# A decoder trunk's squared-ReLU MLP: reordering its first, middle and last steps

## The chip, the cores and the metric

The kernel runs on one core of one Trainium2 chip. The metric is the device time of one execution in microseconds. A core has five engines that run side by side, each working through its own instructions strictly in the order in which they were queued: TensorE (PE in the profile, with its weight loads as PEld), VectorE (DVE), ScalarE (ACT), GpSimd (POOL) and SyncE (SP), which here only issues DMAs. They wait for one another through semaphores. What an engine does after an instruction that waits has to wait too, even if its own data are there.

## The reference

The input is 1024 tokens of 1024 features. There are two layers. Each adds three terms to the residual stream x: a token mixer (a convolution block in layer 0, forgetting attention, "FoX", in layer 1), cross-attention into 256 memory tokens, and the MLP. The change is about the MLP, what comes just before it (the memory attention) and what comes just after the first one (FoX):

```python
def rmsnorm(x, g):
    y = x * lax.rsqrt(jnp.mean(x * x, axis=-1, keepdims=True) + RMS_EPS)
    return y * g

def sqrelu_mlp(h, w1, w2):                       # 1024 -> 4096 -> 1024
    return jnp.square(jax.nn.relu(h @ w1)) @ w2

# per layer l
x = x + memory_cross_attention(rmsnorm(x, norm_mem_g[l]), ...)
h = rmsnorm(x, norm_ff_g[l])
x = x + sqrelu_mlp(h, ff_w1[l], ff_w2[l])
# before layer 1: k, v, gates from rmsnorm(x, kv_norm_g) @ kvf_w; q from rmsnorm(x, norm_mix_g[1]) @ fox_wq
```

## The kernel before

**Layout and precision.** Features lie on the 128 partitions: x is kept as 16 tiles `X[:, c, half]` of 128 x 512 (8 chunks of features by 2 halves of the tokens). Each product is made three times, to keep accuracy: an operand is split into a rounded high part (made by ACT, a copy to the rounded type) and a low part, the rest (made by DVE: source minus high part, line 153, `low`). Three matmuls, low by high, high by low and high by high, then go into the same bank of PSUM (`passes`, `product`).

**The MLP as a list of steps.** `mlp` (line 581) does each of its two products with the seven-product scheme for 2 by 2 blocks (Strassen-Winograd): instead of eight products of quarter blocks it needs seven, and pays with sums of quarters. `steps` (line 636) is one list of 226 entries (weight group g, which weight piece b11, b21, t1 ..., which quarter of the operand a11, a12, s1 ..., which PSUM bank, its pool). One step is 12 matmuls: 4 chunks by 3 passes. Steps 0 to 15 are done the plain way, for groups 0 and 1, while the quarter sums s1 to s4 of x are not there yet: steps 0 to 7 use the first half of the tokens (a11, a12), steps 8 to 15 the second (a21, a22). From step 16 on, 14 steps serve two groups: groups 2 to 15 make the inner activation u (steps 16 to 113), groups 16 to 31 multiply it by the second weight (steps 114 to 225).

**The order of the work is written out by hand.** `at(n, f)`, `at_once(n, f)` and `at_end(n, f)` put a piece of work before, first before, or after step n. The loop at line 1011 goes through the steps and issues, for each n: the work put before it, the high part of the weight of step n+5 (ACT, line 628), its low part for step n+4 (DVE, line 632), the 12 matmuls (line 1026), and the work put after it. The context `in_order` (line 995 to 1031) fixes this order on every engine, SP among them. Weights of the seven-product scheme are themselves sums: `combine` (POOL, line 622) makes t1 to t4 of a group from its raw pieces, t1 = b12 - b11, t2 = b22 - t1, and so on. The raw pieces of a group come in two loads, `load_raw(g, 0)` with b11 and b21 and `load_raw(g, 1)` with b12 and b22, into two buffers for each of the two.

**The first steps.** The sum of squares of the second half of the tokens is made when the loop is about to begin (line 1010: 8 Squares on ACT, 7 additions on DVE, line 188). After step 0, PE takes its mean over the features (line 163), DVE and POOL make the inverse root, and after step 1 PE spreads it over the partitions (line 172). From step 2 on, DVE scales the second half (line 674), ACT and DVE split it, and POOL makes the quarter sums in place, four instructions for each chunk c = 0 to 3 (`sum_second`, line 689). Their high parts (ACT, line 704) stand at step 6 + c and their low parts (DVE, line 709) at 7 + c; s4 follows at 14 and 15. After step 15 the memory of x is given up for 16 buffers "u" (`open_up`), and ACT takes the first results out of PSUM into them (line 842).

**The middle.** u and its quarter sums go through memory in HBM: `store` and `low_inner` write them, `load_inner` reads them back as operands of the second product, in four parts f = 0 to 3 of four groups each. a11 and a12 are stored already split (high and low). s1 to s4 and a22 are stored once and split again when read: `high_of_inner` (ACT, line 910) and `low_of_inner` (DVE, line 914). For the first part, f = 0, the loads stand at steps 102, 104, ... 114, in the order a11, a12, s2, s3, s1, a22, s4, and the splits of s2 at 108 and 110, of s1 at 112 and 113, of s4 at 116 and 117. The raw weights b12 and b22 of groups 16 and 17 are loaded at 110 and 111. In the second product, a bank holds first a11's product; ACT copies it (`copy_first`, line 924) before a12's product is added into it, which is why steps 116 and 117 wait for the copies of 114 and 115.

**The last steps, and FoX.** In the last 14 steps (212 to 225) the results are added to x (DVE, line 934), squared (ACT, line 970) and summed (DVE, line 978) for the next norm. The mean of the first half is taken after step 222, its spread after 223. `fox_layer` (line 1035) then scales and splits the first half (line 216 on DVE, 218 on ACT, 153 on DVE), and multiplies it by the first pieces of wk and fox_wq (line 259) and by the gate weights; the second half of x follows. `projections` (line 1157) goes on from there; it asks for the first piece of wv when it is at the second entry of its list.

## Time and profile before

| | |
|---|---|
| median of 3 timed runs (lowest to highest) | 2849.24 us (2848.0 to 2851.68) |
| the profiled execution: time, span | 2853.82 us, 2852.0 us |
| PE busy, of the span | 2749.8 us, 96% |
| DVE, ACT, POOL busy | 71%, 45%, 28% |
| matmuls of the two MLPs (line 1026) | 5424, 1253.8 us |
| mean granted TensorE clock | 0.988 |

The stages follow one another on PE: convolution and memory matrices to 517 us or so, memory attention, the first MLP (713 to 1361 us), FoX (to about 1980 us), memory attention, the second MLP (2185 to 2836 us), the last norm. A row of a group reads: line, engine, operation, tile written <- tiles read, shapes, count | busy time, mean duration in ns of one | idle time of the engine just before these instructions, and what ended it. Idle time counts only on the engine that bounds a stage; here that is PE almost everywhere. A row of a stretch (from:to in us) reads: length, busy time of PE, PEld, DVE, ACT and POOL with the number of instructions, then the TensorE clock that was granted (1.00 is full), the share of time in which the DMA engines were busy, and what they moved.

### The profile page before, as it was taken

The page shows a single profiled execution, that of the slowest core. Times are in us where ns is not written, and L with a number is a line of the kernel's source. Part 1 is how long each engine was busy: PE and PEld are TensorE (multiplying, and loading weights), DVE is VectorE, ACT ScalarE, POOL GpSimd, SP SyncE. Part 2 cuts the span into 40 slices and gives each one's busy share as a digit, 9 for nine tenths or more (in the row PEclk, how much of TensorE's full clock was granted, in tenths as well). Part 3 has the DMA queues.
Part 4 walks back from the last instruction along what each step waited for, and adds up shares of the span by engine and source line. Part 5 has one row for each costly group of instructions (what it writes and reads, how often), then busy time and mean ns, then how long its engine had stood idle before and what let it go on. Part 6 is the DMA issues. An engine that isn't in the chain of part 4 may idle for free.

```text
span 2852.0 us, 36295 instructions
## 1 busy us (share of the span) xinstructions
PE 2749.8 (96%) x12968; PEld 2265.0 (79%) x12968; DVE 2038.1 (71%) x3295; ACT 1276.7 (45%) x2293; POOL 809.7 (28%) x537
## 2 busy tenths in 40 slices
PE   8999999999899999999799999989999999999998
PEld 6777877888688878888588888878887788878886
DVE  5999983644775576777788888875545865677776
ACT  5112143533465553334466666673433555543332
POOL 0000000000666544774000000000000766635763
PEclk9999999999999999999999999999999999999999
DMA  6334463222165576552222221243213355565651
GB/s 217 118 118 133 136 201 118 86 89 85 42 216 178 189 285 209 211 199 96 67 62 72 64 64 54 68 135 103 94 56 104 117 201 179 198 228 203 225 197 62
DMA packets 165429, 390.68 MB, mean 137 GB/s; under 512 B 17265, under 2 KB 46193, under 8 KB 164993
## 3 DMA queue, kind: packets, MB, share of 16 engines
q1 hardware_dynamic: 165248, 388.37, 40.4%
q8 instruction: 102, 1.67, 0.2%
q14 instruction: 79, 0.64, 0.1%
HBM read 270.79 MB, written 113.31 MB: 135 GB/s over the span
## 4 chain that ended last, share of the span: by engine, by line
PE 74%; DVE 11%; ACT 5%; DMA 4%; issue 3%; POOL 2%; SPq 0%; DVEq 0%; POOLq 0%; ACTq 0%
PE mm L1026 36%; PE mm L259 27%; PE mm L1182 5%; DVE op L153 2%; POOL x L689 2%; DVE x L398 1%; DVE w L153 1%; PE mm L1268 1%; DVE x L1237 1%; PE mm L1280 1%; PE mm L1281 1%; ACT x L1242 1%; DMA raw<-mqk 1%; DVE both L390 1%; PE mm L1232 1%
## 5 line engine op out<-in xcount | busy, mean ns | idle before, releaser
L1026 PE MATMUL mm<-op,w 128*128 128x512 f32 x5424 | 1253.8, 393 | 31.5 <-DVE w L153 11.1
L1026 PEld LDWEIGHTS mm<-op,w 128*128 128x128 f32 x5424 | 1027.0, 190 | 255.0 <-ACT m L924 11.5
L259 PE MATMUL mm<-op,wh 128*128 128x512 f32 x1056 | 329.1, 393 | 0.7 <-DVE op L153 0.7
L153 DVE TENSOR_TENSOR w<-r,w 128x512 fp32r<-128x512 f32 x264 | 267.4, 1017 | 33.5 <-ACT w L628 33.5
L203 POOL TENSOR_TENSOR r<-v,mhalf 128x4 f32<-128x4 f32 (+1 forms) x17 | 18.8, 1106 | 928.1 <-DVE v L201 928.1
L628 ACT CAST w<-r 128x512 fp32r<-128x512 f32 x264 | 162.7, 622 | 259.8 <-PE mm L1026 195.1
L259 PEld LDWEIGHTS mm<-op,wh 128*128 128x128 f32 x1056 | 198.9, 189 | 45.7 <-DVE op L153 4.0
L1182 PE MATMUL mm<-op,wh 128*128 128x512 f32 x736 | 230.3, 394 | 0.0
L153 DVE TENSOR_TENSOR w<-t,w 128x512 fp32r<-128x512 f32 x180 | 178.4, 1003 | 65.0 <-ACT w L628 64.8
L259 PE MATMUL mm<-op,wl 128*128 128x512 f32 x528 | 210.0, 399 | 12.7 <-ACT op L218 8.3
L622 POOL TENSOR_TENSOR t<-r,t 128x512 f32<-128x512 f32 x120 | 194.2, 1618 | 95.1 <-DVE w L153 53.8
L156 ACT CAST wh<-raw 128x1024 fp32r<-128x1024 f32 x96 | 100.8, 1051 | 197.2 <-PE mm L259 121.9
L628 ACT CAST w<-t 128x512 fp32r<-128x512 f32 x180 | 112.0, 622 | 151.8 <-PE mm L1026 133.4
L622 POOL TENSOR_TENSOR t<-r,r 128x512 f32<-128x512 f32 x60 | 95.1, 1585 | 290.8 <-DMA r<-in_ff_w 209.8
L934 DVE TENSOR_TENSOR x<-mm,x 128x512 f32<-128x512 f32 x160 | 109.5, 684 | 94.3 <-PE mm L1026 77.6
L830 POOL TENSOR_TENSOR u<-u 128x512 f32<-128x512 f32 x112 | 160.3, 1455 | 6.5 <-ACT u L840 3.0
L1182 PEld LDWEIGHTS mm<-op,wh 128*128 128x128 f32 x736 | 138.8, 189 | 26.6
L259 PE MATMUL mm<-op,xsh 128*128 128x512 f32 x512 | 158.0, 393 | 0.1
L1182 PE MATMUL mm<-op,wl 128*128 128x512 f32 x368 | 154.7, 420 | 2.5 <-DVE wl L153 2.5
L156 ACT CAST pth<-mm 128x512 fp32r<-128x512 f32 (+1 forms) x224 | 105.9, 495 | 109.0 <-PE mm L546 80.8
L398 DVE SCALAR_TENSOR_TENSOR x<-d,par,x 128x512 f32<-128x512 f32 x232 | 154.6, 746 | 0.0
L1242 ACT ACTIVATE x<-x,nb 128x128 f32<-128x128 f32 (+7 forms) x128 | 99.5, 778 | 109.6 <-DVE nb L1240 102.9
(179 smaller groups left out, 4754.3 us busy)
## 6 DMA issues: line engine op xcount, KB each, us to landing
r<-in_ff_w SPq DMA_DIRECT2D x128, 512.0 KB, 4.0
op<-ua SPq DMA_DIRECT2D x80, 512.0 KB, 6.9
us<-u SPq DMA_DIRECT2D x128, 256.0 KB, 3.0
op<-us SPq DMA_DIRECT2D x64, 512.0 KB, 5.5
raw<-mvo SPq DMA_DIRECT2D x32, 512.0 KB, 3.3
ua<-ul SPq DMA_DIRECT2D x64, 256.0 KB, 2.1
ua<-uh SPq DMA_DIRECT2D x60, 256.0 KB, 2.2
raw<-in_pw SPq DMA_DIRECT2D x24, 512.0 KB, 4.8
```

Source lines behind the costliest of these rows:

```text
L153: dve.tensor_tensor(lo, src, hi.bitcast(F32), op=ALU.subtract)
L156: act.copy(hi, src)
L259: pe.matmul(out_ps, x, y, start=i == 0, stop=i == len(terms) - 1)
L398: dve.scalar_tensor_tensor(out[s], d[:, j : j + n], w, y, op0=ALU.mult, op1=ALU.add)
L622: pool.tensor_tensor(t, raws[g, x], raws[g, y], op=ALU.subtract)
L628: act.copy(highs[n][0], raws[steps[n][:2]])
L689: pool.tensor_tensor(out, x1, x2, op=op_)
L830: eng.tensor_tensor(u[g, x], y1, y2, op=op_)
L934: dve.tensor_tensor(v, sums[key], v, op=ALU.add)
L1026: pe.matmul(sums[key], y, z, start=first and i == 0, stop=n == last_of[key] and i == len(terms) - 1, skip_group_check=True,)
L1182: pe.matmul(t, x, y, start=n == 0, stop=n == len(terms) - 1)
L1242: act.activation(x[:, :n], x[:, :n], AF.Exp, bias=nb, accum_out=rs)
```

## The change

It has these parts.

1. **Early sum of squares.** `mem_attention` squares each chunk of the second half as soon as it is final and returns the sum (`seconds`); the sum at line 1010 is gone.
2. **Steps 0 to 15.** Group 1 goes first and group 0 second; in steps 8 to 15 group 0 comes first (its weights are still there from steps 4 to 7) and group 1 last, with its four pieces in another order. The two raw buffers are now tied to g % 2 by name. The raw weights of group 2 are loaded at 4 and 5 (2 and 3 before), those of group 3 at 10 and 12 (10 and 10).
3. **Copies paced by the quarter sums.** The high parts of chunk c = 0 to 3 stand at steps 7, 10, 12 and 14, the low parts one step later; all of s4 at 15. Group 3's t1 and t2 are made at 15 instead of 12.
4. **Middle.** For the first part (groups 0 to 3), s1 and s2 are split when they are made, at steps 29 to 40, and stored as high and low (`ue`), in place of the plain stores; they are read back split, with two loads for one. Their splits at 108 to 113 are gone. Until they are split they stay in their u buffers. Of the last group of the first product, s3 moves from 113 and 114 to 115.
5. **Next norm within the last steps.** For the first MLP, the scaling and splitting of the first half for FoX is put into steps 224 and 225 and after 225 (`start_fox`, `ending`).
6. **FoX** asks for the first piece of wv right after the second half has been scaled and split.

```diff
+    def add_squares(acc, ch):
+        sq = nrm.tile([P, HALF], F32, name="sq", tag="t", bufs=4)
+        act.activation(sq, ch, AF.Square)
+        if acc is None:
+            return sq
+        dve.tensor_tensor(acc, acc, sq, op=ALU.add)
+        return acc
...
                     add_to_x(m, sl, t)
+                    if sl is HALVES[1]:
+                        sums = add_squares(sums, X[:, m, sl])
+            return sums
...
+        ue = {x: dram.tile([P, 2, 4, HALF], F32, name=f"ue{x}{layer}") for x in ("s1", "s2")}
...
-                r = pw.tile([P, NCH, P], F32, name=f"r{j}")
+                r = raw_tiles[g % 2][j]
...
-            for g in range(2):
+            for g in (1, 0):
                 steps += [
...
-            for g in (1, 0):
-                for b, x, c in (("b11", "a21", "c21"), ("b12", "a21", "c22"), ("b21", "a22", "c21"), ("b22", "a22", "c22")):
-                    if g:
-                        again[len(steps)] = {"b11": 4, "b21": 5, "b12": 6, "b22": 7}[b]
-                    steps.append((g, b, x, (g, c), pm if g else ps))
+            seconds_of = (("b11", "a21", "c21"), ("b12", "a21", "c22"), ("b21", "a22", "c21"), ("b22", "a22", "c22"))
+            for b, x, c in seconds_of:
+                again[len(steps)] = {"b11": 4, "b21": 5, "b12": 6, "b22": 7}[b]
+                steps.append((0, b, x, (0, c), pm))
+
+            for b, x, c in (seconds_of[k] for k in (0, 2, 1, 3)):
+                steps.append((1, b, x, (1, c), ps))
...
-                second["r"] = rms_of_sums(second["acc"], RMS_EPS)
+                second["r"] = rms_of_sums(seconds, RMS_EPS)
...
-            for c in range(4):
-                at(6 + c, highs_of_sums, c, ("s2", "s3", "s1"))
-                at(7 + c, lows_of_sums, c, ("s2", "s3", "s1"))
-            at(14, open_operand, "s4")
-            for c in range(4):
-                at(14 + c // 2, highs_of_sums, c, ("s4",))
-                at(15, lows_of_sums, c, ("s4",))
-            at(2, load_raw, 2, 0)
-            at(3, load_raw, 2, 1)
+            for c, n in enumerate((7, 10, 12, 14)):
+                at(n, highs_of_sums, c, ("s2", "s3", "s1"))
+                at(n + 1, lows_of_sums, c, ("s2", "s3", "s1"))
+            at(15, open_operand, "s4")
+            for f in (highs_of_sums, lows_of_sums):
+                for c in range(4):
+                    at(15, f, c, ("s4",))
+            at(4, load_raw, 2, 0)
+            at(5, load_raw, 2, 1)
             at(10, load_raw, 3, 0)
-            at(10, load_raw, 3, 1)
+            at(12, load_raw, 3, 1)
...
-                        at(b - 4 + late, combine, g + i, t)
+                        at(b - 1 if g + i == 3 else b - 4 + late, combine, g + i, t)
...
+            for n, g in ((29, 0), (31, 1), (37, 2), (39, 3)):
+                for i, x in enumerate(("s2", "s1")):
+                    split_inner_at(n + i, g, x)
...
-                        at(b + 13 + i, inner_sums, g + i, NEW[:3], dve)
-                        at(b + 15, inner_sums, g + i, NEW[3:], dve)
+                        at(b + 13 + i, inner_sums, g + i, NEW[:2], dve)
+                        at(b + 15, inner_sums, g + i, NEW[2:], dve)
...
+            def split_before(f, x):
+                return f == 0 and x in ue
...
-                    if x in SPLIT_FIRST:
+                    if x in SPLIT_FIRST or split_before(f, x):
                         for i in range(2):
-                            nc.sync.dma_start(t[:, i].bitcast(F32), ud[x][:, i, k, :])
+                            nc.sync.dma_start(t[:, i].bitcast(F32), (ud if x in SPLIT_FIRST else ue)[x][:, i, k, :])
...
+            def begin_next():
+                for n, f in ending(second["rb"]):
+                    at(end - n, f)
+            if ending is not None:
+                at(b + 12, begin_next)
...
-                second["acc"] = sum_of_squares([X[:, c, HALVES[1]] for c in range(NCH)])
...
+    def start_fox(rb, hs):
+        h = {}
+        def first(c):
+            if c == 0:
+                hs.extend(operands())
+            h[c] = nrm.tile([P, HALF], F32, name="h", tag="t", bufs=4)
+            dve.tensor_tensor(h[c], X[:, c, HALVES[0]], rb, op=ALU.mult)
+            act.copy(hs[c][0][:, HALVES[0]], h[c])
+        def second(c):
+            hi, lo = (y[:, HALVES[0]] for y in hs[c])
+            low(lo, h.pop(c), hi)
+        todo = [(first, 0)]
+        for c in range(1, NCH):
+            todo += [(first, c), (second, c - 1)]
+        todo.append((second, NCH - 1))
+        at = [2] * 4 + [1] * 4 + [0] * (len(todo) - 8)
+        return [(n, partial(f, c)) for n, (f, c) in zip(at, todo)]
...
-                normalize(hs, None, HALVES[0], firsts)
...
                 normalize(hs, None, HALVES[1], rb)
+                ws.append(weights(a["wv"][0], gain="kv"))
...
-            if 0 < j < len(order) - 1:
+            if 1 < j < len(order) - 1:
```

More of the change, by code (lines that the diff above doesn't have):

```diff
@@ L552, in mem_attention @@
             late = None
+            sums = None
             for sl in HALVES:
@@ L578, in mem_attention, with mlp @@
                     add_to_x(m, sl, t)
-    def mlp(layer, copy=None):
+                    if sl is HALVES[1]:
+                        sums = add_squares(sums, X[:, m, sl])
+            return sums
+    def mlp(layer, seconds, copy=None, ending=None):
         nonlocal X, xpool
@@ L605, in operand @@
                 return [(t[:, 0, i, :], t[:, 1, i, :]) for t in ts for i in range(2)], ts
+            raw_tiles = [
+                [pw.tile([P, NCH, P], F32, name=f"r{i}{j}", bufs=1) for j in range(2)] for i in range(2)
+            ]
             def load_raw(g, j):
@@ L811, in low_inner @@
                 low(lo, u[g, x], hi)
+                if x in ue:
+                    del u[g, x]
                 for i, y in enumerate((hi, lo)):
-                    nc.sync.dma_start(ud[x][:, i, g, :], y.bitcast(F32))
+                    nc.sync.dma_start((ue if x in ue else ud)[x][:, i, g, :], y.bitcast(F32))
             def split_inner_at(n, g, x):
@@ L833, in store_rest @@
                 for x in ("a22", "s1", "s2", "s3", "s4"):
-                    store(g, x)
+                    if g >= 4 or x not in ue:
+                        store(g, x)
             def first_outputs(g, names, square):
@@ L845, in mlp @@
             at_end(15, open_up)
-            at_end(15, first_outputs, 0, ("c11", "c12"), False)
-            at(16, first_outputs, 1, ("c11", "c12"), False)
-            at(16, first_outputs, 1, ("c21", "c22"), False)
-            at(17, first_outputs, 1, ("c11", "c12", "c21", "c22"), True)
-            at(18, first_outputs, 0, ("c21", "c22"), False)
-            at(18, first_outputs, 0, ("c11", "c12", "c21", "c22"), True)
-            for g, n in ((1, 18), (0, 23)):
+            at_end(15, first_outputs, 1, ("c11", "c12"), False)
+            at(16, first_outputs, 0, ("c11", "c12"), False)
+            at(16, first_outputs, 0, ("c21", "c22"), False)
+            at(17, first_outputs, 0, ("c11", "c12", "c21", "c22"), True)
+            at(18, first_outputs, 1, ("c21", "c22"), False)
+            at(18, first_outputs, 1, ("c11", "c12", "c21", "c22"), True)
+            for g, n in ((0, 18), (1, 23)):
                 at(n, inner_sums, g, NEW, pool)
@@ L946, in mlp @@
                 for x, ns in (("s2", (8, 10)), ("s1", (12, 13)), ("s4", (16, 17)), ("s3", (19, 20)), ("a22", (22, 23))):
-                    for j, n in enumerate(ns):
+                    for j, n in enumerate(() if split_before(f, x) else ns):
                         at(lb + n, high_of_inner, f, x, j)
@@ L991, in mlp @@
             at_end(b + 11, spread_second)
+            def begin_next():
[3 more added lines that the diff above has]
+                at(b + 12, begin_next)
             with in_order():
                 store_x(0)
-                for g in range(2):
+                for g in (1, 0):
                     for j in range(2):
@@ L1009, in mlp @@
                     fetch_low(n)
-                second["acc"] = sum_of_squares([X[:, c, HALVES[1]] for c in range(NCH)])
                 for n in range(len(steps) + 1):
-                    for f in urgent[n] + before[n]:
+                    for f in chain(urgent[n], before[n]):
                         f()
@@ L1032, in mlp, with fox_layer @@
         return second["rb"], accs[1]
-    def fox_layer(xd, firsts, seconds):
+    def start_fox(rb, hs):
[15 more added lines that the diff above has]
+        return [(n, partial(f, c)) for n, (f, c) in zip(at, todo)]
+    def fox_layer(xd, hs, seconds):
         nonlocal X, xpool
@@ L1291, in trunk @@
         conv_layer(pm, chain(*(memory_matrices(*pools, l) for l in range(2))))
-    mem_attention(0)
+    seconds = mem_attention(0)
     xd = dram.tile([P, NCH, S], F32, name="xd")
-    firsts, seconds = mlp(0, copy=xd)
-    fox_layer(xd, firsts, seconds)
-    mem_attention(1)
-    firsts, seconds = mlp(1)
+    first_normalized = []
+    firsts, seconds = mlp(0, seconds, copy=xd, ending=lambda rb: start_fox(rb, first_normalized))
+    fox_layer(xd, first_normalized, seconds)
+    seconds = mem_attention(1)
+    firsts, seconds = mlp(1, seconds)
     for sl in HALVES:
```

3 lines of the change are left out of this document (1 added, 2 removed).

## The prediction

> **What bounds the kernel now.** First the page: which engine has no time left.
>
> ```profile
> span 2852.0 us, 36295 instructions
> ...
> PE 2749.8 (96%) x12968; PEld 2265.0 (79%) x12968; DVE 2038.1 (71%) x3295; ACT 1276.7 (45%) x2293; POOL 809.7 (28%) x537
> ```
>
> PE bounds it, and no matmul is removed, so the change can only give back PE's idle time and the slow matmuls that follow it. The groups of PE say where it idles in the stages that the change touches:
>
> ```profile
> L1026 PE MATMUL mm<-op,w 128*128 128x512 f32 x5424 | 1253.8, 393 | 31.5 <-DVE w L153 11.1 <-ACT m L924 10.6 <-ACT u L842 4.8
> ...
> L259 PE MATMUL mm<-op,wl 128*128 128x512 f32 x528 | 210.0, 399 | 12.7 <-ACT op L218 8.3 <-DVE wl L153 3.5 <-DVE ol L1284 0.9
> ```
>
> Then I counted 12 matmuls to a step through line 1026 and asked for the stretches in which steps take long. Columns: length; busy time of PE, PEld, DVE, ACT, POOL; granted clock; DMA share; GB/s.
>
> ```profile
> 676.00:712.00 36.00, 35.86 (x171) 29.88 (x169) 12.29 (x14) 8.09 (x10) 0.00 (x0) 1.00 0.49 168
> 713.33:728.16 14.83, 10.74 (x40) 8.73 (x41) 7.78 (x13) 5.37 (x10) 1.32 (x1) 0.77 0.17 55
> 741.00:767.00 26.00, 22.00 (x90) 17.42 (x88) 23.22 (x16) 9.26 (x17) 23.91 (x15) 0.93 0.00 1
> 755.48:766.96 11.48, 7.48 (x26) 5.39 (x24) 11.34 (x9) 3.88 (x8) 9.96 (x7) 0.85 0.00 0
> 769.85:779.59 9.74, 7.32 (x25) 5.59 (x24) 8.60 (x7) 5.79 (x12) 7.88 (x5) 0.82 0.11 43
> 785.23:812.58 27.35, 27.35 (x121) 22.63 (x121) 21.69 (x26) 17.02 (x32) 19.06 (x14) 1.00 0.70 257
> 1046.50:1058.88 12.38, 7.89 (x25) 6.03 (x24) 12.35 (x11) 8.42 (x14) 9.24 (x6) 0.72 0.28 98
> 1360.77:1389.31 28.54, 17.55 (x64) 12.56 (x65) 16.54 (x25) 6.91 (x11) 1.01 (x1) 0.82 0.23 70
> 2185.32:2199.85 14.53, 10.44 (x41) 8.53 (x41) 7.77 (x13) 5.36 (x10) 1.32 (x1) 0.77 0.16 55
> 2227.18:2238.66 11.48, 7.36 (x25) 5.31 (x23) 11.34 (x9) 3.88 (x8) 9.97 (x7) 0.85 0.01 1
> 2241.54:2251.03 9.49, 7.13 (x26) 5.48 (x25) 8.41 (x7) 5.58 (x11) 7.58 (x5) 0.82 0.11 44
> 2518.13:2532.42 14.29, 8.17 (x26) 6.24 (x24) 14.22 (x13) 10.05 (x16) 10.37 (x6) 0.78 0.32 119
> ```
>
> The undisturbed row, 785.23, gives the measure: 121 matmuls in 27.35 us at full clock, 2.72 us a step. Each disturbed stretch of a MLP holds two steps, 5.44 us; the first (713.33) also a mean and a spread, some 2.0 us together at full clock:
>
> ```profile
> 1350.48 1.05 PE mm L163 x8
> ...
> 1354.40 0.89 PE mm L172 x8
> ...
> 1381.28 7.38 PE mm L259 x24
> ```
>
> So these are lost: steps 0-1, 7.4 us (second MLP 7.1); steps 12-13, 6.0 (6.0); steps 15-16, 4.3 (4.1); steps 115-116, 6.9 (8.9). FoX's start (1360.77) holds two products of 24 matmuls, a mean and a spread, 12.9 us, and loses 15.7. Together 66: the most that there is to win. A good part of it isn't idle time but matmuls at a lower clock (0.72 to 0.85 in these rows).
>
> **Steps 0 and 1.** The chain of waits there:
>
> ```profile
> 712.52 2.47 DVE w L153 x4
> ...
> 719.68 0.70 DVE acc L188
> 720.42 1.72 PE mm L163 x8
> ```
>
> PE's mean after step 0 waits for the last addition of the sum of squares, which DVE can only begin behind the weight splits. The change moves 8 Squares and 7 additions under the second half's output product, where DVE is busy 12.3 of 36 us and ACT 8.1 (row 676.00): seven additions of 0.70 are 5 us, hidden. The mean then waits for nothing and both losses go: 7.4 + 7.1 = 14.5 us. What is late next is the first weight: if the last chunk's Square and addition stand ahead of it on DVE, step 0 begins up to 1.4 us later (two instructions of 0.70). I take 0.4 in each MLP, since the splits are ready earlier. Sum: 13.7, bounds 11.7 and 14.5.
>
> **Steps 12 to 19.** Here DVE waits for ACT, ACT for POOL's quarter sums, and weights queue behind.
>
> ```profile
> L689 POOL TENSOR_TENSOR x<-x,x 128x512 f32<-128x512 f32 x13 | 20.6, 1594 | 0.8
> L153 DVE TENSOR_TENSOR op<-x,op 128x512 fp32r<-128x512 f32 x12 | 19.2, 1648 | 4.0 <-ACT op L704 3.7
> ```
> ```profile
> 770.34 1.14 ACT L628 CAST w<-r 128x512 fp32r<-128x512 f32 x2 [6.41 <-DMA r<-in_ff_w]
> ```
>
> Steps 15-16 wait for ACT, which waits 6.41 us for group 3's raw weights; their buffer was held to the end of the plain steps. Paced copies put up to three weights ahead of each quarter's splits, and the new buffer order brings group 2's weights at 4 and 5. That cures steps 12 to 16. But DVE's work stays: from the first quarter's sums (741.0, 12.8 us after step 2 begins at 728.16) to the weight of step 19 it has 12 splits, 4 of s4 and 8 weights, 24 instructions. They took 1.65 us beside POOL, against 0.69 in FoX's start, where POOL idles (row below). POOL has 13 sums and now, with no wait between, 7 weight differences: 20 x 1.65 = 33 us. DVE passes one beside each and the last four at about 0.6: 12.8 + 33 + 2.4, with a late first split, makes 48.7 us. PE wants step 19 at 17 x 2.72 = 46.2. So a gap of 2.5 us stays. The stretch 769.85 prices such a gap: ACT u L842, 4.8 for two, so 2.4 idle, and 4.3 lost; 1.9 went to the clock. I take 2.5 + 1.9 = 4.4 in each MLP: 20.4 lost before (6.0 + 4.3 + 6.0 + 4.1), 8.8 after, gain 11.6. Bounds: no gap, 20.4; DVE at 1.65 throughout, a gap of 6.2 and 3 more of clock, 2.
>
> [...] The row 769.85 shows 0.82 of the clock after 2.4 us of idling, so I keep the price from the row.
>
> **The middle.** Here I expect no gain.
>
> ```profile
> 1028.71 6.31 DMA op<-us
> ...
> 1035.04 1.06 ACT op L910
> ```
> ```profile
> 1037.98 0.33 SPq L615 DMA_DIRECT2D r<-in_ff_w  x1
> ```
> ```profile
> 1045.39 1.57 POOL L622 TENSOR_TENSOR t<-r,r 128x512 f32<-128x512 f32 x1 [0.86 <-DMA op<-ua]
> 1047.04 1.63 POOL L622 TENSOR_TENSOR t<-r,t 128x512 f32<-128x512 f32 x1
> ```
> ```profile
> 1048.70 0.62 ACT L628 CAST w<-t 128x512 fp32r<-128x512 f32 x1
> ...
> 1052.05 0.63 ACT L767 ACTIVATE u<-u 128x512 f32<-128x512 f32 x1 [2.73 <-DVE u L785]
> ...
> 1053.25 0.57 ACT L924 COPY m<-mm 128x512 f32<-128x512 f32 x1
> ```
> ```profile
> DMA packets 5044, 14.72 MB, mean 368 GB/s; under 512 B 560, under 2 KB 560, under 8 KB 5040
> ...
> q1 hardware_dynamic: 5040, 14.68, 95.9%
> ...
> us<-u SPq DMA_DIRECT2D x8, 256.0 KB, 8.3
> ```
>
> ACT waits for s2 to land, all its queue slips, and PE waits at step 116 for `copy_first` (1053.25). The change takes s2's and s1's splits out (4 of 1.06 on ACT, as many on DVE) and with them ACT's wait for s2. But ACT has another appointment in front of that copy: the high part of step 119's weight, t2 of group 17 (1048.70). It began as POOL finished t2 (1047.04 + 1.63 = 1048.67), and POOL began when group 17's b12 and b22 had landed. That load, issued at 1037.98, stands behind s2 and s1 in SP's order, in a stretch where the DMA engines are 95.9% busy. Reading s2 and s1 split adds four loads of 512 KB ahead of it. At 14.72 MB in 40 us and that share, one takes 1.3 us: 5.2 us later. Then t2 is ready at 1053.9, its cast 0.6 later, two activations and the copy (1052.05 to 1053.82) 1.8 after that: step 116 begins at 1056.2, where it began at 1053.87. I take the stall as 2.4 us longer, in both MLPs: -4.8. Bounds: the loads hide, and 6.9 + 8.9 = 15.8 come back; or -10.4, the whole 5.2 twice.
>
> **Steps 23 to 42.** Eight splits at 29 to 40 (0.62 on ACT, up to 1.65 on DVE) and eight more stores; s1 and s2 hold up to four of the 16 u buffers for some ten steps longer. DVE has 5.7 of 27 us free there (785.23) and weights run four steps ahead, so most hides; 8 x 1.65 = 13 us over twelve steps (33 us) about uses up what is free. I take 1 us in each MLP: -2; bounds 0 and -8.
>
> **FoX.**
>
> ```profile
> L153 DVE TENSOR_TENSOR op<-h,op 128x512 fp32r<-128x512 f32 x8 | 5.5, 686 | 0.2
> L216 DVE TENSOR_TENSOR h<-x,mm 128x512 f32<-128x512 f32 x8 | 5.4, 680 | 0.0
> ...
> L246 DVE TENSOR_TENSOR raw<-raw,par 128x1024 f32<-128x1024 f32 x3 | 3.7, 1222 | 6.0 <-DMA raw<-in_wk 3.2 <-DMA raw<-in_wv 2.7
> ```
> ```profile
> L1182 PE MATMUL mm<-op,wl 128*128 128x512 f32 x368 | 154.7, 420 | 2.5 <-DVE wl L153 2.5
> ```
>
> The spread ends at 1355.3 (1354.40 + 0.89). From there DVE has 16 instructions of 0.68 for the first half, five of 0.7 for the last results and squares and two of 1.2 for wk: 16.8 us, to 1372. PE follows one operand behind, to 1373; the second piece of weights (1.2, a cast, 1.2) lets the second product begin at 1375.5, where it began at 1381.28. Gain 6; bounds 3 (DVE also waits for a load, 2.7 in the row) and 12. wv's earlier split can remove the 2.5 us before line 1182; I take 1, since attention's first scores also wait for the gates and for key copies, which nothing speeds up. Together 7.
>
> **Sum.** 13.7 + 11.6 - 4.8 - 2 + 7 = 25.5. The profiled execution took 2853.82 us (span 2852.0); 2828.3 after. The median of the three runs, 2849.24, lies 4.6 lower: 2824. Its own range is 2813 to 2836.
>
> **Rivals.** *The middle is cured* (the four loads hide or the copy comes first): for it speaks that ACT goes on the moment s2 lands (1028.71 + 6.31, and 1035.04), against it the full DMA row. 4.8 + 15.8 more: 2803. Chance 0.25.
>
> [...] Chance 0.15.
>
> *Slower*: the u buffers. s1 and s2 wait for their splits, stores queue for 8.3 us to land, as in the DMA row, and the next results find no buffer, so that ACT and DVE stand still ahead of the weights. It decides once PE loses over 12.8 us in each MLP between steps 23 and 42. Two pairs of stores in a row at 6.3 us of landing (1028.71), less the four steps of lead, 10.9, twice (29 to 32, 37 to 40), and 3 us of clock each time: 2 x 2 x (12.6 - 10.9 + 3) = 19, still faster; with landings of 8.3 us, 2 x 2 x (16.6 - 10.9 + 3) = 35: 2858. Chance 0.08.
>
> **Chances.** The forecast 0.52. Run to run this kernel can't tell less than about 0.2%, 5.7 us, from no change: faster means under 2843.5. [...] Faster 0.85, same 0.07, slower 0.08. The range from 2799 to 2842 leaves out the slower case and both tails.
>
> **What would show it.** In the profile after: PE's idle time at line 163 gone; steps 12 to 18 at 2.72 us and a gap of 2 to 3 us before step 19, with DVE w as releaser; at step 116 still a wait for line 924, with ACT's cast of t behind POOL and group 17's load landing some 5 us later; FoX's first product beginning right after step 225. The forecast is wrong if step 116 starts without a wait, if no gap stands before step 19, or if steps 23 to 42 lose over 3 us.

## The result: 1.0% slower, and the profile after

The changed kernel took 2879.95 us (median of 4 runs, 2876.05 to 2881.16), the kernel before, beside it on the same chip, 2850.46 us (2848.0 to 2853.67): a ratio of 1.0100, 95% interval 1.0083 to 1.0118. Forecast were 2824 us and a range up to 2842. The profiled execution took 2881.16 us, 27.3 more than that of before.

The page of the changed kernel, its first lines:

```profile
span 2879.4 us, 36352 instructions
...
PE 2746.9 (95%) x12968; PEld 2266.0 (79%) x12968; DVE 2051.4 (71%) x3303; ACT 1278.7 (44%) x2301; POOL 811.4 (28%) x537
```

PE's work is what it was (2749.8 us before); all of the loss is waiting. The groups of PE say where (after the busy time and the mean duration: idle time just before, and what ended it; the MLP's matmuls, line 1026 before, are now on line 1063, line 259 is now 268):

```profile
L1063 PE MATMUL mm<-op,w 128*128 128x512 f32 x5424 | 1249.5, 392 | 55.3 <-DVE w L153 21.9 <-ACT m L955 15.8 <-ACT u L867 9.2
...
L268 PE MATMUL mm<-op,wl 128*128 128x512 f32 x528 | 210.2, 399 | 10.0 <-ACT op L1081 4.8 <-DVE wl L153 4.3 <-DVE ol L1342 0.9
...
L163 PE MATMUL mm<-mean_col,acc 128*128 128x1 f32 x100 | 14.6, 266 | 17.1 <-DVE acc L188 16.1 <-DVE acc L353 1.0
```

Before the MLP's matmuls there are 55.3 us of idling instead of 31.5. In front of a mean (line 163) that waits for line 188's additions on DVE stand 16.1 us; that row had 8.2 before. But then it was the sum over the second half, which the change takes away; now it is the sum over the *first* half, which it doesn't touch. The stretches of the changed kernel (length; busy PE, PEld, DVE, ACT, POOL; clock; DMA share; GB/s):

```profile
709.03:733.38 24.35, 3.94 (x17) 3.59 (x17) 17.31 (x28) 12.80 (x22) 1.01 (x1) 0.60 0.03 11
733.38:742.69 9.31, 9.31 (x40) 7.76 (x41) 3.02 (x6) 1.24 (x3) 1.32 (x1) 0.77 0.19 55
761.00:778.17 17.17, 17.17 (x77) 14.21 (x76) 17.17 (x11) 8.68 (x16) 16.62 (x11) 1.00 0.19 62
778.17:797.68 19.51, 13.50 (x49) 9.72 (x47) 15.70 (x14) 9.63 (x20) 13.03 (x9) 0.91 0.18 58
1058.95:1074.82 15.87, 8.17 (x25) 6.19 (x24) 11.58 (x11) 8.59 (x14) 10.03 (x7) 0.70 0.65 243
```

The first row is new: from the last product of the memory attention to the first of the MLP, 24.35 us in which PE does 3.94. In the kernel before PE idled 1.47 us there:

```profile
713.33 3.00 PE L1026 MATMUL mm<-op,w 128*128 128x512 f32 x12 [1.47 <-DVE w L153]
```

The other rows are steps 0 and 1 (9.31 us, 14.83 before), a stretch without loss that holds steps 12 to 14, steps 15 to 18 (19.51 us, 15.38 before), and steps 115 and 116 (15.87 us, 12.38 before).

PE's timeline of that first row (start, length, instruction, idle time before it and its releaser):

```profile
717.08 1.87 PE L163 MATMUL mm<-mean_col,acc 128*128 128x1 f32 x8 [8.05 <-DVE acc L188]
720.35 2.07 PE L172 MATMUL mm<-ident,r 128*128 128x128 f32 x8 [1.40 <-POOL r L212]
733.38 2.04 PE L1063 MATMUL mm<-op,w 128*128 128x512 f32 x4 [10.96 <-DVE w L153]
```

Three waits, 8.05 + 1.40 + 10.96 = 20.4 us: sum, inverse root, scaling and splitting of the first half, one after the other, with PE standing by. On ACT, the last of the early Squares (line 194) comes first, and the first half's Squares (184, 187) right behind it:

```profile
709.86 0.63 ACT L194 ACTIVATE sq<-x 128x512 f32<-128x512 f32 x1 [4.81 <-DVE x L289]
710.39 0.61 ACT L184 ACTIVATE acc<-x 128x512 f32<-128x512 f32 x1
710.91 1.14 ACT L187 ACTIVATE t<-x 128x512 f32<-128x512 f32 x2
```

In the kernel before, the same eight Squares stood one by one behind the weight casts of the second half's memory attention, some 97 to 128 us earlier (the first two and the last are shown):

```profile
582.66 0.63 ACT L184 ACTIVATE acc<-x 128x512 f32<-128x512 f32 x1
...
585.55 0.63 ACT L187 ACTIVATE t<-x 128x512 f32<-128x512 f32 x1
...
618.26 0.62 ACT L187 ACTIVATE t<-x 128x512 f32<-128x512 f32 x1
```

So the kernel before did the first half's norm ahead, under the memory attention of the second half, and the changed one can't any more. The first MLP begins 20.05 us later, the second another 20.4 (from the end of the first MLP to the start of the second it takes 16.55 us more, although FoX gains 3.9 there). What the steps gain doesn't make up for it.

**Theory A**: all these tiles have one tag, t, with four buffers, and buffers are handed out in the order in which the code is traced. The early Squares are traced ahead of the first half's sum and ask for eight of them, one for each chunk; the first half's `acc` gets one only behind the last of these, however long its data have been there. **Rival Q**: the norm is late because of its place in the queues of ACT and DVE or its priority. **Rival E**: the early Squares themselves are the work that PE waits for. **Rival M**: the loss comes from the other parts of the change.

### The profile page after: what moved, and what is told of

It reads as the page before. It is cut to its first block, busy times and chain, and to the rows that moved or that the text cites. A ratio compares the mean times of both kernels' runs of the same rounds, so it can differ in the third digit from the quotient of the medians.

```text
span 2879.4 us, 36352 instructions
## 1 busy us (share of the span) xinstructions
PE 2746.9 (95%) x12968; PEld 2266.0 (79%) x12968; DVE 2051.4 (71%) x3303; ACT 1278.7 (44%) x2301; POOL 811.4 (28%) x537
## 4 chain that ended last, share of the span: by engine, by line
PE 71%; DVE 17%; ACT 4%; DMA 3%; issue 3%; POOL 1%; SPq 0%; DVEq 0%; POOLq 0%; ACTq 0%
PE mm L1063 36%; PE mm L268 24%; PE mm L1240 5%; DVE x L407 4%; DVE op L153 3%; DVE both L399 2%; DVE w L153 2%; PE mm L1326 1%; DVE x L1295 1%; ACT x L1300 1%; PE mm L1338 1%; PE mm L1339 1%; DVE wl L153 1%; PE mm L1290 1%; DMA mqk<-o 1%
## 5 line engine op out<-in xcount | busy, mean ns | idle before, releaser
L1063 PE MATMUL mm<-op,w 128*128 128x512 f32 x5424 | 1249.5, 392 | 55.3 <-DVE w L153 21.9
L153 DVE TENSOR_TENSOR w<-r,w 128x512 fp32r<-128x512 f32 x264 | 278.6, 1060 | 27.2 <-ACT w L648 27.2
L212 POOL TENSOR_TENSOR r<-v,mhalf 128x4 f32<-128x4 f32 (+1 forms) x17 | 18.8, 1104 | 957.3 <-DVE v L210 957.3
```

What stands on the lines that cost most here:

```text
L153: dve.tensor_tensor(lo, src, hi.bitcast(F32), op=ALU.subtract)
L1063: pe.matmul(sums[key], y, z, start=first and i == 0, stop=n == last_of[key] and i == len(terms) - 1, skip_group_check=True,)
```

## The experiments

Edits are on the changed kernel where nothing else is said; line numbers shift by a few between kernels. Ratios are to the kernel before, run on the same chip.

**Part one undone (no_early).**

```diff
-                    if sl is HALVES[1]:
-                        sums = add_squares(sums, X[:, m, sl])
...
+                second["acc"] = sum_of_squares([X[:, c, HALVES[1]] for c in range(NCH)])
                 for n in range(len(steps) + 1):
```

> Part one of the change undone: the second half's sum of squares stands in the MLP again, all else is as in the changed kernel. Theory A: the start of the MLP gains 2 x 19 us back, steps 0 and 1 lose 5.5 and 5.9 us again: 2880 - 38 + 11 = 2853, within 5; so the first part costs 27 us and all the others together bring nothing (the kernel before: 2850). Rival M (the loss sits in the middle or in FoX, and the start of the MLP is only shifted): over 2870.

2850.15 us, 0.9993 (0.9983 to 1.0002): M falls. Part one cost 30 us; the other parts together gave about 2, and the interval reaches zero.

**Part one alone (early_alone)**: the kernel before, with `add_squares` as the change has it and nothing else.

> The kernel before with the first part of the change alone, as the change writes it (early squares in the shared tiles, the first half's norm traced behind them). Theory A: this part carries the whole loss by itself. By the traces of before and after the MLPs begin 20 us later each and steps 0 and 1 gain 5.5 and 5.9 us: 2852 + 40 - 11 = 2881, between 2874 and 2888. Rival (the loss needs the other parts too, the new buffer order or the new order of groups): under 2862.

2881.36 us, 1.0106 (1.0091 to 1.0121), with waits of 8.05, 1.41 and 10.96 us before the first MLP: the whole loss, from this part alone.

**High priority (prio).**

```diff
-                rb = spread(inverse_rms([X[:, c, HALVES[0]] ...
+                with tc.high_priority(offset=100000):
+                    rb = spread(inverse_rms([X[:, c, HALVES[0]] ...
```

> The changed kernel with the first half's sum of squares, mean and spread at high priority, so that they may pass whatever is ready in a queue; tiles and traced order stay. Theory A: a priority can't bring a tile that is still held, 2880 within 6, gaps of 8 and 11 us before the MLP as before. Rival Q (order in the queues): the norm moves under the memory attention, 2844, within 6.

2881.55 us (one run), with waits of 8.05, 1.40 and 10.96 us: nothing moved, as theory A has it. By itself that is weak, since a priority without any effect would look the same.

**Tiles of their own (own_tiles, own_all).** The early Squares got tiles in the memory attention's own pool, and their mean moved to that stage's end.

```diff
-        sq = nrm.tile([P, HALF], F32, name="sq", tag="t", bufs=4)
+        sq = p.tile([P, HALF], F32, name="sq", tag="sq", bufs=2)
...
-            return sums
+            return rms_of_sums(sums, RMS_EPS)
```

> The early squares and their sum take tiles of their own (a tag in the memory attention's pool) instead of the four shared tiles of tag t; the mean then stands at the end of the memory attention. Theory A (tiles are handed out in the order in which the code is traced; the first half's sum comes later in that order and can't get a tile before the last early square gives one up, so its norm can't be done ahead): the first half's Squares lie under the memory attention again, at about 582 to 620 us, PE's gaps of 8.05, 1.40 and 10.96 us before the MLP go, all but some 2 us for the last square, its addition and the mean: 2880 - 2 x 18 = 2844, between 2838 and 2850. Rival Q (the norm is late because the early squares stand ahead of it in the queues of ACT and DVE, whatever the tiles): still 2880, within 6.

2866.67 us, 1.0050 (1.0033 to 1.0066): outside the ranges of both, between them. The first half's Squares did go back, to 584.0 us, with their order in the code as in the changed kernel, so it was the tiles that had held them, and Q, which had them late whatever the tiles, falls:

```profile
L184 ACT ACTIVATE acc<-x x1: 629/629/629, 584.0 to 584.0; 128x512 f32<-128x512 f32 x1
```

But on PE their mean did not:

```profile
712.36 0.38 PE L163 MATMUL mm<-mean_col,sq 128*128 128x1 f32 x2 [2.23 <-DVE sq L197]
712.61 1.03 PE L163 MATMUL mm<-mean_col,acc 128*128 128x1 f32 x8
713.50 0.81 PE L163 MATMUL mm<-mean_col,sq 128*128 128x1 f32 x6
716.69 2.08 PE L172 MATMUL mm<-ident,r 128*128 128x128 f32 x8 [2.38 <-POOL r L212]
729.63 2.93 PE L1063 MATMUL mm<-op,w 128*128 128x512 f32 x6 [10.87 <-DVE w L153]
```

The first half's mean (acc) stands in the midst of the second's (sq), though its sum was done some 90 us before. The same thing again, one tile further: the means and spreads share two PSUM banks and a few small tiles, and the second half's mean is now traced ahead. In own_all it got a bank of the attention's pool and small tiles of its own:

```diff
+    def mean_apart(p, acc):
+        m = bank(p)[:, :4]
...
+        v = nrm.tile([P, 4], F32, name="v2", bufs=1)
...
+        r = nrm.tile([P, 4], F32, name="r2", bufs=1)
```

> As own_tiles (early squares with tiles of their own, 2866.7 us), and the second half's mean has a PSUM bank and two small tiles of its own too, instead of the two banks of the pool ps that the first half's mean and spread also use. In own_tiles the Squares had moved ahead (584 us) but the first half's mean still stood at 712.6, beside the second's. Theory A in full (every tile, PSUM's too, is handed out in traced order): now the first half's mean, spread and splits move under the memory attention as well, the 10.87 us before the first product of the MLP go, only the wait for the last addition stays: 2867 - 2 x 11 = 2845, between 2840 and 2851. Rival Q (the means are kept in order by PE's queue): 2866 within 6.

2853.35 us (one run), outside the range that theory A gave. Its mechanism is there: the first half's mean is taken at 621.0 us, and the wait of 10.87 us is 0.96.

```profile
L163 PE MATMUL mm<-mean_col,acc x8: 250/250/271, 621.0 to 621.8; 128*128 128x1 f32 x8
```
```profile
714.82 1.05 PE L218 MATMUL mm<-mean_col,sq 128*128 128x1 f32 x8 [2.23 <-DVE sq L197]
716.83 5.44 PE L1073 MATMUL mm<-op,w 128*128 128x512 f32 x16 [0.96 <-DVE w L153]
```

The first MLP starts 12.8 us earlier than in own_tiles. The missing 8 us are spread over the MLPs, where an undisturbed step takes 2.75 instead of 2.72 us (steps 30 to 112 of the first: 228.07 us, in the next kernel 225.76). The edit can hardly be the cause of that: in this one execution matmuls that follow one another take 1% longer from the start, in stages that no edit touches, with a mean granted clock of 0.991 over the execution (0.988 in that of the kernel before). The last 383 matmuls of the convolution, in the kernel before and here:

```profile
428.38 89.50 PE mm L259 x383
```
```profile
427.84 90.59 PE mm L278 x383
```

One per cent of the two MLPs is some 13 us (an estimate from these rows), more than what is missing. Why this execution was slower is open; the other 18 traces have the pace of the first row.

**The order in the code (norm_ahead).** Tiles as in the changed kernel; the first half's sum and mean are traced before the early Squares:

```diff
+                if sl is HALVES[1]:
+                    first = inverse_rms([X[:, c, HALVES[0]] for c in range(NCH)], RMS_EPS)
                 early = [(weights(vd[m]), bank(pm)) for m in range(2)]
...
-                rb = spread(inverse_rms([X[:, c, HALVES[0]] for c in range(NCH)], RMS_EPS))
+                rb = spread(first)
```

> The shared tiles stay, but the first half's sum of squares and mean are traced ahead of the second half's output product, so ahead of the early squares. Theory A: the tiles come free in time, the gaps of 20.4 us before each MLP shrink to the 1.5 us of the kernel before, and steps 0 and 1 keep their gain: 2880 - 2 x 19 = 2842, between 2836 and 2848. Rival E (the early squares themselves, eight Squares and seven additions, are what PE waits for): over 2868.

2842.21 us, 0.9965 (0.9953 to 0.9977): faster than the kernel before, and 38 us faster than the changed one, by moving one request ahead of the others. The early Squares are all still there, so E falls. In front of the MLP PE now waits once:

```profile
716.81 3.00 PE L1066 MATMUL mm<-op,w 128*128 128x512 f32 x12 [2.92 <-DVE w L153]
```

**The first term by itself (early_ahead)**: the kernel before with part one and norm_ahead's order.

> The kernel before with the first part of the change alone (early squares of the second half), and with the first half's sum and mean traced ahead of them as in norm_ahead. Nothing else of the change. Prediction's first term as it was meant (steps 0 and 1 gain 13.7 us, nothing else moves), less the 1.5 us by which norm_ahead's first step began later, twice: 2851 - 13.7 + 3 = 2840, between 2836 and 2845. If the first term itself is wrong (the squares cost time elsewhere): 2851 within 4.

2845.29 us, 0.9972 (0.9961 to 0.9983): a gain of 7.7 us, just short of the expected range. Steps 0 and 1 together gain 4.8 us in the first MLP and 4.5 in the second, and the first step's wait grows from 1.47 to 2.92 us. They gain less than in norm_ahead, where they take 3.65 + 3.62 us, because step 0 takes 6.44 here (last section).

**Steps 15 to 18**, from norm_ahead. In the changed kernel PE waits three times, each time for ACT:

```profile
781.91 3.02 PE L1063 MATMUL mm<-op,w 128*128 128x512 f32 x12 [0.86 <-ACT u L867]
788.66 4.61 PE L1063 MATMUL mm<-op,w 128*128 128x512 f32 x12 [3.74 <-ACT u L867]
794.60 3.58 PE L1063 MATMUL mm<-op,w 128*128 128x512 f32 x13 [1.33 <-ACT u L798]
```

ACT's Relu (line 867), which empties a bank into a u tile, waits for DVE's splits: u lies where x lay, and x is still being split.

```profile
788.01 0.60 ACT L867 ACTIVATE u<-mm 128x512 f32<-128x512 f32 x1 [6.15 <-DVE op L153]
791.50 2.06 ACT L867 ACTIVATE u<-mm 128x512 f32<-128x512 f32 x4 [2.89 <-DVE op L153]
```

Either the wrong chunk of x is split last (theory X), or DVE has too much to do beside POOL (theory P). First come two other orders (reverse, outer_first), then POOL's weight differences for groups 2 and 3 are left out (no_combine), then moved to DVE (combine_dve):

```diff
-                    normalized(c, 1, second["rb"], ("a21", "a22"))
+                    normalized(3 - c, 1, second["rb"], ("a21", "a22"))
...
-            for c, n in enumerate((7, 10, 12, 14)):
+            for c, n in zip((3, 2, 1, 0), (7, 10, 12, 14)):
```

> On norm_ahead (2842.2 us): the four chunks of the second half are normalized, summed and split in the order 3, 2, 1, 0 instead of 0, 1, 2, 3; the same instructions otherwise. Theory X (at steps 15 to 17 PE waits for a bank, the bank for the Relu that empties it, and the Relu for its u tile, which lies on the part of x whose last split comes last, chunk 3): with chunk 3 first the tiles come free early, the gaps of 0.85, 3.74 and 1.32 us at steps 15 to 17 go, with the slow matmuls behind them 8 us in each MLP: 2826, between 2820 and 2832. Rival P (DVE is simply full there, 24 instructions of 1.77 us beside POOL, in whatever order): the gaps move to another step, 2842 within 5.

2836.8 us, 0.9940 (0.9925 to 0.9955): between the two ranges, just short of P's, so it decides little. The three gaps became one of 4.23 us before step 16; steps 15 to 18 took 17.7 us instead of 19.5.

outer_first is the same with the order 3, 0, 2, 1:

> On norm_ahead (2842.2 us): the chunks of the second half in the order 3, 0, 2, 1, s4's splits in the order 3, 2, 1, 0. In norm_ahead the second Relu waited for chunk 3's last split, in reverse the first one waited for chunk 0's. Theory X (the first u tiles lie where chunks 0 and 3 of x lay, and whichever of these is split last holds the Relus that empty the banks for steps 16 and 17): with both first, the first two Relus start at once, the gaps at steps 15 to 17 shrink from 5.9 us to under 2, and the time falls by 12 to 16 us: 2829, between 2825 and 2833. Rival P (DVE is full there in whatever order): 2838 within 4, like reverse.

2840.52 us, 0.9953 (0.9936 to 0.9971), as P has it. The first two Relus start at once, as X said, but the third waits, and PE behind it:

```profile
759.37 1.08 ACT L871 ACTIVATE u<-mm 128x512 f32<-128x512 f32 x2
767.84 2.07 ACT L871 ACTIVATE u<-mm 128x512 f32<-128x512 f32 x4 [7.39 <-DVE op L153]
```
```profile
770.95 4.63 PE L1067 MATMUL mm<-op,w 128*128 128x512 f32 x10 [5.19 <-ACT u L802]
```

X names the right tile, but a new order only moves the wait to step 18.

```diff
             def combine(g, name):
+                if g in (2, 3):
+                    raws[g, name] = raws[g, "b12"]
+                    return
```

> On norm_ahead (2842.2 us): the weight differences of groups 2 and 3 are left out of POOL's work (eight instructions of about 1.7 us in each MLP; the weights b12 stand in for them, so these products are not the reference's). The splits of chunk 3 and of s4 then run without POOL beside them. Theory P and theory X together: a split takes 0.68 instead of 1.77 us after the last quarter sum, the third Relu starts some 7 us earlier, the gaps at steps 15 to 17 nearly go: 2842 - 2 x 7 = 2828, between 2822 and 2834. Rival Z (DVE's length beside POOL is not the cause): gaps as before, 2842 within 5.

2833.69 us, 0.9929 (0.9914 to 0.9943): 8.5 us less than norm_ahead. The gaps at 15 to 18 are gone but for 0.30 us, and those steps take 11.9 us instead of 19.5. Not all of that shows in the time: there is a new wait of 2.38 us before step 28, and step 0, which this edit doesn't touch, takes 5.2 us instead of 3.65 (last section). With the differences moved instead of left out:

```diff
-                pool.tensor_tensor(t, raws[g, x], raws[g, y], op=ALU.subtract)
+                eng = dve if g in (2, 3) else pool
+                eng.tensor_tensor(t, raws[g, x], raws[g, y], op=ALU.subtract)
...
-                        at(b - 1 if g + i == 3 else b - 4 + late, combine, g + i, t)
-                    at(b - 1, combine, g + i, "t3")
+                        at({2: 14, 3: 16}.get(g + i, b - 4 + late), combine, g + i, t)
+                    at({2: 17, 3: 18}.get(g + i, b - 1), combine, g + i, "t3")
```

> On norm_ahead (2842.2 us): the weight differences of groups 2 and 3 (eight in each MLP) are done by DVE instead of POOL, at steps 14 to 20, so that POOL idles while DVE splits the last chunk and s4. Theory P (beside POOL's instructions each of DVE's takes 1.77 instead of 0.68 us, and that is what delays the third Relu, wherever the order puts it): DVE gets eight instructions more and yet is done earlier, 20 x 0.68 = 13.6 us instead of 12 x 1.77 = 21.2; the gaps at steps 15 to 17 shrink from 5.9 us to under 2, the time by 5 to 8 us in each MLP: 2829, between 2824 and 2835. Rival N (DVE's number of instructions is what counts): the gaps grow, 2842 or more.

2829.28 us, 0.9928 (0.9910 to 0.9945). In this kernel, and in best3 below, the fourth difference stands at 19 and 20, behind the next groups' load, so it is made of their weights, and what these two kernels compute is not the reference; the amount of work is the same. With that difference back at 16 and 17, the weights are the right ones:

> The same correction on combine_dve (2829.3 us), without ue_off. Theory P: 2829, between 2824 and 2835; gaps at steps 15 to 17 under 2 us in sum, against 5.9 in norm_ahead. Rival N (number of DVE's instructions): 2842 or more.

2829.36 us, 0.9918 (0.9900 to 0.9937). The last seven splits of x, in the changed kernel (first line) and here:

```profile
782.86 8.61 DVE L153 TENSOR_TENSOR op<-x,op 128x512 fp32r<-128x512 f32 x7
```
```profile
763.16 4.30 DVE L153 TENSOR_TENSOR op<-x,op 128x512 fp32r<-128x512 f32 x7
```

There are eight instructions more on DVE in each MLP, and the splits take half the time: POOL is busy for 6.17 of the 8.61 us in the first row, and for none of the 4.30 in the second. Steps 15 to 18 take 13.3 us instead of 19.5 (10.9 without any loss), and gaps of 0.59 and 1.00 us are left. P holds.

**The middle**, from norm_ahead. The changed kernel, on SP: group 16's raw weights, the four loads of s1, group 17's raw weights.

```profile
1047.37 0.33 SPq L635 DMA_DIRECT2D r<-in_ff_w  x1
1049.28 3.45 SPq L934 DMA_DIRECT2D op<-ues  x4
1053.09 0.33 SPq L635 DMA_DIRECT2D r<-in_ff_w  x1
```

and on POOL, ACT and PE:

```profile
1063.83 1.67 POOL L642 TENSOR_TENSOR t<-r,r 128x512 f32<-128x512 f32 x1 [3.87 <-DVE u L854]
1065.58 1.59 POOL L642 TENSOR_TENSOR t<-r,t 128x512 f32<-128x512 f32 x1
```
```profile
1067.20 0.62 ACT L648 CAST w<-t 128x512 fp32r<-128x512 f32 x1 [4.75 <-POOL t L642]
...
1068.92 0.57 ACT L955 COPY m<-mm 128x512 f32<-128x512 f32 x1
```
```profile
1069.54 5.06 PE L1063 MATMUL mm<-op,w 128*128 128x512 f32 x11 [7.70 <-ACT m L955]
```

It is the chain of the forecast, link by link: group 17's load, issued at 1053.09, lands at 1063.67 us, and POOL begins at 1063.83. Its row names an addition on DVE instead, which ended at almost the same moment, 1063.78; in norm_ahead the same wait is put down to the load. PE ended steps 114 and 115, and with them the product that the copy reads, at 1061.83 (1053.74 + 8.09); the copy, behind the cast on ACT, begins at 1068.92. The test (raw_first) puts group 17's load ahead of s1's:

```diff
-                        at(b - 6 + i + 2 * late, load_raw, g + i, 1)
+                        at(b - 6 + (0 if late else i) + 2 * late, load_raw, g + i, 1)
```

> On norm_ahead (2842.2 us): the load of group 17's b12 and b22 stands in SP's order right behind group 16's, ahead of the four loads of s1. Theory L (the loads in front of it make group 17's second difference late, its cast holds up copy_first on ACT, and PE waits at step 116): the load lands 4 to 5 us earlier (1046.5 in norm_ahead), the gap of 9.28 us before step 116 shrinks to 4 or 5, and the time falls by 4 to 5 us in each MLP: 2833, between 2829 and 2837. Rival S (the copy is late because of ACT's own work or of the s1 operands, which now land later): no gain, 2842 within 4.

2833.54 us, 0.9932 (0.9916 to 0.9949). The two loads stand together, t2's cast begins at 1046.21 instead of 1050.13 us in norm_ahead, and the wait before step 116 falls from 9.28 to 4.73 us (norm_ahead's row is the first, the others are raw_first's):

```profile
1052.47 3.78 PE L1066 MATMUL mm<-op,w 128*128 128x512 f32 x8 [9.28 <-ACT m L958]
```
```profile
1029.98 2.33 SPq L638 DMA_DIRECT2D r<-in_ff_w  x2
```
```profile
1048.55 7.74 PE L1066 MATMUL mm<-op,w 128*128 128x512 f32 x20 [4.73 <-ACT m L958]
```

And the early splits undone (ue_off, from norm_ahead):

```diff
             def split_before(f, x):
-                return f == 0 and x in ue
+                return False
...
-            for n, g in ((29, 0), (31, 1), (37, 2), (39, 3)):
-                for i, x in enumerate(("s2", "s1")):
-                    split_inner_at(n + i, g, x)
```

> On norm_ahead (2842.2 us): s2 and s1 of the first four groups are stored whole and split after loading again, as in the kernel before; the splits at steps 29 to 40 and the four loads more go. Theory L: group 17's load moves up by four loads of about 1.3 us, but ACT again waits for s2, so that steps 115 and 116 lose what they lost in the kernel before, 6.9 and 8.9 us, instead of 11.7 and 10.6 us: 2842 - 6.5 = 2836, between 2831 and 2840. Rival (early splits pay, as the change has them): over 2846.

2826.54 us, 0.9904 (0.9889 to 0.9919): this part of the change loses 16 us where 6.5 were expected. Steps 115 to 117 account for 11.6: 19.9 to 16.5 us in the first MLP, 18.8 to 10.6 in the second. The second does much better than in the kernel before (17.4), with loads and splits as they were there. The link that differs is the same load: it lands 0.78 us after step 114 begins, in the kernel before 3.10 us after it, and in ue_off's own first MLP 3.75. It was issued earlier by as much; what moves SP's queue by some 3 us there is open. So a part of that gain may be luck; the rest of the 16 us lies within the two intervals.

**Together.** best2 is norm_ahead, outer_first, ue_off and raw_first; best3 norm_ahead, ue_off and combine_dve; best4 the same with combine_dve2.

> The changed kernel with norm_ahead, outer_first, ue_off (s2 and s1 split after loading, as before) and raw_first together. By the single steps: 2842 - 13 (outer_first, as expected of it) - 16 (ue_off as measured, 2826.5) - 2 (raw_first, of which ue_off already has most: two loads of 1.3 us in front of it instead of four) = 2811, between 2806 and 2824: better than both kernels. If the gains overlap (each only lets the next wait be seen): 2824 or more.

2832.43 us, 0.9921 (0.9908 to 0.9934): not better than ue_off alone. Steps 17 and 18 take 8.08 and 5.29 us as in outer_first, and the second MLP's steps 115 to 117 are back at 16.4.

> norm_ahead with ue_off (2826.5 us) and combine_dve together. If the two stages are apart, as the traces say (steps 12 to 19 and steps 115 to 117): 2826.5 - 13 = 2813, between 2808 and 2821. If the middle takes back what the first steps gain, as best2 (2832.4, with outer_first and raw_first) did not gain on ue_off: 2826 within 5.

2819.56 us, 0.9892 (0.9875 to 0.9910): 9.7 us less than combine_dve, from which it differs by ue_off alone.

> norm_ahead with ue_off and the weight differences of groups 2 and 3 on DVE, as best3 (2819.6 us), but with the fourth difference at steps 16 and 17, ahead of the next groups' loads, so that each product has its own weights. The load at step 17 now has to wait for that difference. If the wait hides (it did in the kernel before, where POOL made it): 2820, between 2814 and 2825, better than both kernels. If the later load matters: 2826.

2818.1 us (2817.16 to 2821.49), 0.9884 (0.9869 to 0.9899): 1.2% faster than the kernel before, 2.1% faster than the changed one, and 11.3 us less than combine_dve2, again by ue_off alone. PE idles 19.8 us before the MLP's matmuls, 55.3 in the changed kernel:

```profile
L1063 PE MATMUL mm<-op,w 128*128 128x512 f32 x5424 | 1241.5, 391 | 19.8 <-ACT m L955 6.0 <-DVE w L153 5.8 <-DVE x L965 3.1
```

## Why the prediction was wrong

The step that failed is the first: "hidden". The Squares were hidden, as forecast (they run from 674.5 to 709.9 us, beside the output product), and the mean behind step 0 no longer waits. But that sentence of the forecast priced the moved instructions by their engines' free time alone, and not by the four tiles that they take. The question that the forecast asked, what is late next, it answered with "the first weight", up to 1.4 us; late next was the whole norm of the first half, 20 us. The trace of before showed that this norm ran at 582 to 620 us, so that it had a lead to lose, and the code showed the tag that it shares with the new tiles. None of the rivals had it; the one that ended slower put the loss on the u buffers.

By terms, from the two profiled executions:

| | forecast, us | measured, us |
|---|---|---|
| start of the two MLPs | (0.4 each, in the next row) | +20.05, +20.4 |
| steps 0 and 1 | -13.7 | -5.5, -5.9 |
| steps 12 to 18, to the start of 19 | -11.6 | -2.1, -2.0 |
| steps 19 to 114 | +2 | 0 |
| steps 115 to 117 | +4.8 | +3.9, +1.5 |
| FoX, to its first scores | -7 | -3.9 |
| sum | -25.5 | +26.5, of 27.3 |

**Steps 0 and 1.** The mechanism was right, the size a little high: 11.4 us of the 14.5 that were lost came back. What the forecast took at 0.4 us, the first weight behind the last Square and addition, comes to 1.45 us in each MLP once the norm is ahead again (norm_ahead waits 2.92 us instead of 1.47), which is the bound that it had named.

**Steps 12 to 19.** Steps 12 and 13 are cured (5.44 us for both, 11.48 before). That DVE's work would stay was right as well, and so was the reason, POOL beside it. Mis-sized was what is left: forecast 4.4 us in each MLP, as a gap before step 19; it is 8.6, at steps 15 to 18. In its sum, 12.8, 33 and 2.4 make 48.2 and not 48.7: the 0.5 us for a late first split have no row behind them, which changes nothing here. The forecast let DVE's queue fall behind the weights; but the first to need DVE's splits are the Relus, since they write where x lies, and PE needs their banks three steps earlier. The lower bound, a gain of 2 with DVE at 1.65 us throughout, which the rival of chance 0.15 took, was closer than 11.6 (measured 4.1). That POOL's work holds DVE up is what combine_dve2 confirms, 8.61 against 4.30 us for seven splits.

**The middle.** Right in sign, place and chain, and in the sum (5.4 us against 4.8). That the size fits so well is in part luck: it is 3.9 in one MLP and 1.5 in the other, and by the same code steps 115 to 117 take 17.0 to 20.7 us in the kernels that keep this part and the load's place. raw_first shows the load's place to be the cause, and ue_off, best3 and best4 that this part of the change is a loss.

**Steps 19 to 114.** 261.27 us before and after in the first MLP: the splits are hidden and no buffer is missing.

**FoX.** The gap before the first product fell from 8.29 to 4.82 us only. The group row of line 268 in the first section shows it, and that weights (wl) still hold up the products behind it. To the first scores FoX gains 3.9 us in the changed kernel. But that size is not firm: in the 16 traces with the new FoX the first scores come 44.0 to 47.0 us after the end of the MLP, in the three with the old one (before, early_alone, early_ahead) 50.6 to 50.9. That is a gain of 3.7 to 6.9 us, 4.9 in the mean, which lies between the forecast's 7 and the 3 of the rival of chance 0.15 and decides nothing between them.

**Without the failed step** the other terms, as measured, give 2853.82 - 11.4 - 4.1 + 5.4 - 3.9 = 2840, or 2835 with the forecast's step of 4.6 us from the profiled execution to the median. norm_ahead, which is nearly that, but waits 1.45 us longer before each MLP, measured 2842.21. So even then the time would have stood at the upper end of the range or just beyond it, far from 2824: the second thing that the forecast had wrong is the size of steps 12 to 19, 4.1 us gained instead of 11.6.

## What to carry to other kernels

Before you move work earlier, list what it allocates, not only what it executes: a tag's buffers, PSUM banks and small tiles are handed out in the order of the code, so that an early user with late data stands in the way of a later user whose data are long there. See in the trace what already runs ahead of its place in the code, since that is what such a move can take away; the repair may be one line, the order of two requests. And where one engine slows another, as POOL did DVE here (seven splits in 8.61 us beside it, in 4.30 without), reordering moved the wait; taking the work off the first removed most of it, although the other then had more instructions.

## What the runs showed of the hardware beyond that

The same idle time costs the clock in one place and not in another. In all twelve kernels with the first half's norm traced ahead, PE idles 2.92 or 2.93 us before each MLP. In 14 of these 24 places step 0 then takes 3.62 to 3.65 us, in 10 it takes 4.99 to 6.44. Two kernels that do the same up to there, the same four microseconds (reverse, then raw_first):

```profile
714.00:718.00 4.00, 3.65 (x21) 3.17 (x21) 2.62 (x5) 2.60 (x5) 0.00 (x0) 1.00 0.02 4
```
```profile
714.00:718.00 4.00, 3.72 (x9) 2.98 (x10) 2.54 (x5) 1.92 (x4) 0.00 (x0) 0.50 0.02 4
```

21 matmuls at clock 1.00 against 9 at 0.50. A gap of this kind costs 2.92 us or up to 2.8 more. What decides between them is not shown, and nothing in the code up to there tells which, so a forecast can only give both.
